# Keys and values of two heads as paired products, with the block sums and the early logits moved

## The chip, the cores and the metric

The kernel runs on one core of one Trainium2 chip. A core has a matrix engine (TensorE, PE in the profile, with its weight loads as PEld), a vector engine (VectorE, DVE), a scalar engine (ScalarE, ACT), GpSimd (POOL) and SyncE (SP), which here only issues transfers. The metric is the device time of one execution in microseconds (us), over three runs of the kernel before: 1576.21, 1579.66 and 1579.71, so the median is 1579.66 us. The profile is of one further execution.

## The reference

One inference step of one decoder layer. A prompt of 512 tokens (16 learned tokens in front, 528 in all) and 8 decoding sequences of 4 tokens each (32) pass through the same weights, so every projection has 560 rows.

```
h = RMSNorm(x)
[q,k,v,ga | cb,cc,ch,gc | ma,mc] = h @ w_in              # 2048 -> 12288
a = StickBreakingAttn(q,k,v) * silu(ga)                  # 8 heads of 128
c = cb * conv3_causal(cc * ch) * silu(gc)
m = sigmoid(ma + b_ga) * (a @ w_pa) + sigmoid(mc + b_gc) * (c @ w_pc)
y = x + RMSNorm(m @ w_out)
A[t,s] = sigmoid(z_ts) * prod_{s<j<t} (1 - sigmoid(z_tj)),  z = q.k / sqrt(128) + b_head
```

The prompt attends to itself. The decoding tokens attend to 512 cached positions each, four pages of 128 positions from a paged cache, and to their own sequence. Keys and values of all rows are outputs too. Everything is float32.

## The kernel before

**Products.** Each float32 operand is split into a high part and a low part: ACT copies the high part (`whi`, L242), DVE subtracts it from the operand (`wlo`, L243), and PE multiplies high by high, high by low and low by high, so every product of 128 rows takes three matmuls. The normed input stands in `h_hi` and `h_lo`, 16 blocks of 128 rows by 560 columns; its columns are cut in two halves of 280. The weights come as tiles of 1024 by 128 over the SP queue into five buffers (`raw`), and the split tiles have three buffers each (`whi`, `wlo`).

**A plain projection** (`proj`, L258) of 128 columns of `w_in` has two weight tiles and 16 x 3 x 2 = 96 matmuls of 280 columns. Queries use 272 columns of each half.

**A pair** (`pair` and `seven`, L983) makes 256 columns of `w_in` as a 2 by 2 block product in seven products instead of eight (Winograd's form). Each product has 8 x 3 = 24 matmuls. It needs sums of weight blocks (four additions on DVE, L1002 to L1020), and sums of the blocks of `h`: three tiles `t_hi`, `t_lo` pairs, and the block (0,1) of `h` itself is replaced by a sum. The four results leave PSUM one after the other.

**Order of stages.** First the norm and the first queries. Then `head_now` for heads 0 to 3: keys, values, the query projection of head h+4, and the attention of head h for the prompt (`attend`: scores L623, softplus on ACT and DVE, suffix sums on PE L705, exponentials L711, values L717). The attention's tiles lie in the pool `now`. Then `head_later` for heads 4 to 7: keys and values are made and stored for later. Then the block sums (L948 to L968, on DVE and ACT), which are in a pool of their own (`tsum`). The six tiles `t_hi`, `t_lo` are taken right after the pool `now` is given back, on the same side of the memory: 52 KB a partition that stand where `now` (51,968 bytes a partition) stood. From there everything that reads `h` is a pair: 4 pairs for `ga`, 16 for the convolution, 16 for the gates `ma` and `mc` (L1127 to L1156). Then attention of heads 4 to 7 beside `c @ w_pc`, then `a @ w_pa`, `w_out` and the final norm.

**Decoding beside this.** `decode_steps` is a generator. Its first part makes the logits of the cached keys on DVE: 16 units, each with four pages, each page with 16 dot products of 128 by 128 (`junk`, L784). So there are 64 of them in a unit and 1024 in all. The first six units (`DEC1`) run beside heads 0 to 3, in a pool that must be closed before the pool `tsum` opens; the other ten run beside `ga`, the convolution and the first gates (`dec_group` after each pair, numbered n = 1 to 36; the first loads are issued after the second `ga` pair). When all logits are there, two steps make their softplus on ACT (L469 to L472) and the suffix sums; the next makes the exponentials, and then come the values.

**What sets the order.** The instructions of each engine are put in an order when the program is built, by a planner that follows the written order where several are ready and lets later work go ahead where nothing earlier is. On the chip each engine then keeps that order. `pin` (also `keep_in_program_order`) holds an instruction behind the one written before it on its engine; `issue_after` holds a group behind a named one. The sigmoids of the gates (L1145) that are written after a softmax step stand behind the last ACT instruction of that step (L1144), and the step stands behind the four sigmoids written before it (`behind_gates`), so that the ACT tables change seldom.

Of the kernel before, what the change touches and what calls it, by code (L numbers as in the profile page):

```python
# [17 lines left out]
P = 128  # L18
# [28 lines left out]
EPS = 1e-6  # L47
DEC1 = 6
SCRATCH = 4096
FIRST = 4  # L50
WARM = 10
NOW = 4
LNEXP = "natural_log_exp_and_others"
SCALE = P ** -0.5
# [6 lines left out]
def hybrid_step_kernel(  # L61
# [176 lines left out]

    def w_split(x):
        hi = whl.tile([P, 8, P], F32R, tag="hi", name="whi")  # L240
        lo = whl.tile([P, 8, P], F32R, tag="lo", name="wlo")
        act.copy(hi, x)  # L242
        low[0] = dve.tensor_sub(lo, x, hi.bitcast(F32))  # L243
        return hi, lo
# [258 lines left out]

    def natural(raw, nat, nat_s):
# [8 lines left out]
        dve.tensor_copy(nat[0:16, 4, :], pt[0:16, 0:P])  # L513
        dve.tensor_copy(nat_s, pt[0:TS, P:2 * P])

# [47 lines left out]

    def k_proj(h):
        o = proj(GATE_K + h * P, ALL)
        kr = hp.tile([P, T], F32, name="raw", bufs=2)
        for ob, s in nparts(o):
            act.copy(kr[:, s], ob)
        kn = hp.tile([P, 5, P], F32, name="nat", bufs=2)
        ks = hp.tile([TS, P], F32, name="ks", bufs=1)  # L570
        natural(kr, kn, ks)
        outputs(k_prompt, k_sample, h, kn, ks, pin if h == 0 else lambda x: x)

        zz = z_ps()[0:TS, 0:TS]
        pe.matmul(zz, lhsT=kr[:, TP:T], rhs=qs_all[:, h, :], start=True, stop=True)
# [4 lines left out]
    def v_proj(h, pl=None):  # L580
        o = proj(GATE_V + h * P, ALL)
        vr = hp.tile([P, T], F32, name="raw", bufs=2)
        for ob, s in nparts(o):
            act.copy(vr[:, s], ob)
        vn = hp.tile([P, 5, P], F32, name="nat", bufs=2)
        vs = hp.tile([TS, P], F32, name="ks", bufs=1)
        natural(vr, vn, vs)
        outputs(v_prompt, v_sample, h, vn, vs)
        pool.dma_start(v_scr[:, h * P:(h + 1) * P], vs)
        if pl is None:  # L590
            pool.dma_start(vn_scr[h][0:512].rearrange("(a p) d -> p a d", p=P), vn[:, 0:4, :])
            pool.dma_start(vn_scr[h][512:TP], vn[0:16, 4, :])
            return None
        return v_split(pl, vn)

# [8 lines left out]
    def attend(pl, h, khi, klo, vhi, vlo, qhi, qlo, pl_a=None, after=None, between=None):  # L604
# [114 lines left out]
        yield ot  # L719

    def head_now(h):

        qr = hp.tile([P, TQ], F32, name="qr", bufs=2)[:, 0:PQ]
        nc.sync.dma_start(qr, qt_scr[h][:, 0:PQ])
        khi, klo = k_split(np_, k_proj(h))
        dec_step(1 if h else 0, "part")
        vhi, vlo = v_proj(h, np_)
        dec_step(1, "part")
        q_proj(NOW + h)
        dec_step(2, "part")  # L730
        ot = next(attend(np_, h, khi, klo, vhi, vlo, *q_split(np_, qr)))
        dec_step(2, "part")
        at = np_.tile([P, PQ], F32, name="at", bufs=1)
        act.copy(at, ot)
        pool.dma_start(a_scr[h], at)

    def head_later(h):
        pool.dma_start(k_scr[h], k_proj(h))
        dec_step(2, "part")
        v_proj(h)  # L740
        dec_step(2, "part")

# [183 lines left out]
    nctx.close()  # L926
    for h in range(NOW, H):
        head_later(h)
    dec_step(64, "part")
# [5 lines left out]
    for i in range(3):  # L935
        ttp = tctx.enter_context(tc.tile_pool(name=f"tt{i}", bufs=1))
        t_hi.append(ttp.tile([P, 8, HU], F32R, name=f"t_hi{i}"))
        t_lo.append(ttp.tile([P, 8, HU], F32R, name=f"t_lo{i}"))
    h_f, l_f = h_hi.bitcast(F32), h_lo.bitcast(F32)

    def blk(x, i, j):
        return x[:, 8 * i:8 * i + 8, (j + 1) * HC - HU:(j + 1) * HC]

    def t_split(hi, lo, x):
        act.copy(hi, x)
        dve.tensor_sub(lo, x, hi.bitcast(F32))

    with tc.tile_pool(name="tsum", bufs=2, side="right") as tsp:  # L948
        r1 = tsp.tile([P, 8, HU], F32, name="r1", bufs=1)
        for c in range(0, 8, 2):  # L950
            def part(x, *ij):
                return (blk(x, *ij) if ij else x)[:, c:c + 2]

            r, x, y = part(r1), *(tsp.tile([P, 2, HU], F32, name=n) for n in "xy")
            dve.tensor_sub(r, part(h_f, 0, 0), part(h_f, 0, 1))
            dve.tensor_add(r, r, part(l_f, 0, 0))
            dve.tensor_sub(r, r, part(l_f, 0, 1))
            dve.tensor_add(x, r, part(h_f, 1, 1))
            dve.tensor_add(x, x, part(l_f, 1, 1))
            t_split(part(t_hi[0]), part(t_lo[0]), x)  # L960
            dve.tensor_sub(y, part(h_f, 0, 0), x)
            dve.tensor_add(y, y, part(l_f, 0, 0))
            t_split(part(t_hi[1]), part(t_lo[1]), y)
            dve.tensor_sub(x, part(h_f, 1, 0), x)
            dve.tensor_add(x, x, part(l_f, 1, 0))
            t_split(part(t_hi[2]), part(t_lo[2]), x)
        for c in range(0, 8, 2):
            t_split(blk(h_hi, 0, 1)[:, c:c + 2], blk(h_lo, 0, 1)[:, c:c + 2], r1[:, c:c + 2])  # L968
    hctx.close()
# [63 lines left out]
    def pair(c, n):  # L1033
# [6 lines left out]
        def rt(i):  # L1040
            return lambda k: (t_hi[i][:, k, HU - n:HU], t_lo[i][:, k, HU - n:HU])

        ws = blocks_of(win, c)
        s = sp2.tile([P, 8, P], F32, name="s")
        yield from seven(ws, n, rb, rt, s, lambda name: sp2.tile([P, HU], F32, name=name)[:, :n])

    gctx, uctx = ExitStack(), ExitStack()
    sp2 = gctx.enter_context(tc.tile_pool(name="sums", bufs=1))
    gp = gctx.enter_context(tc.tile_pool(name="gates", bufs=2))
    up_ = uctx.enter_context(tc.tile_pool(name="convu", bufs=2))  # L1050
# [89 lines left out]
    for j in range(0, KD, 2):  # L1140
        for w, c in ((0, COL_MA), (1, COL_MC)):
# [384 lines left out]
```

## Time and profile before

| what | value |
|---|---|
| median of three runs | 1579.66 us (1576.21 to 1579.71) |
| the profiled execution | 1577.78 us, span 1576.2 us |
| mean granted TensorE clock | 0.993 |
| PE busy | 1560.4 us, 99% of the span |
| PEld busy | 1526.9 us, 97% |
| DVE busy | 1261.6 us, 80% |
| ACT busy | 753.5 us, 48% |
| POOL busy | 236.2 us, 15% |

The span runs from the first to the last instruction; the execution's own time is 1.6 us longer. Times within the profile are counted from the start of the span. Matmuls are pipelined, so the duration of one (289 ns on average for 272 columns) is not what it costs: that is the distance from one start to the next. A wait is charged to the instruction that came last, as far as the profile can tell.

### The profile page before, as it was taken

How to read it: one execution, taken by the hardware profiler on the slowest of the kernel's cores; microseconds unless marked ns; L12 is line 12 of the kernel's file. 1: busy time of each engine (PE TensorE's matmuls, PEld its weight loads, DVE VectorE, ACT ScalarE, POOL GpSimd, SP SyncE). 2: the span in 40 equal slices, each digit the busy share in tenths (PEclk: the TensorE clock that was granted, in tenths of full speed). 3: DMA queues.
4: the chain of work that ended last, by engine and by line, in shares of the span. 5: the costliest groups of instructions: out<-in, count | busy, mean ns of one | idle time of the engine just before them, and what ended most of it. 6: DMA issues, size and time to landing. Idle time of an engine off the chain costs nothing.

```text
span 1576.2 us, 32342 instructions
## 1 busy us (share of the span) xinstructions
PE 1560.4 (99%) x12172; PEld 1526.9 (97%) x12172; DVE 1261.6 (80%) x3574; ACT 753.5 (48%) x1339; POOL 236.2 (15%) x428
## 2 busy tenths in 40 slices
PE   8999999999999999999999999999999999999997
PEld 8999999999999999999999999898899999999997
DVE  7328999965799999999999996655678857877686
ACT  6235555434444444344444465444476733445562
POOL 1133333222111011011011113212100010000000
PEclk8999999999999999999999999999999999999999
DMA  8245556344564445445355547667595465443345
GB/s 256 86 135 179 165 169 184 107 125 141 155 189 128 143 141 156 134 142 168 108 172 174 168 131 239 188 190 229 156 310 181 129 187 170 148 115 88 102 142 186
DMA packets 300674, 252.77 MB, mean 160 GB/s; under 512 B 11521, under 2 KB 268613, under 8 KB 299701
## 3 DMA queue, kind: packets, MB, share of 16 engines
q1 hardware_dynamic: 272021, 160.45, 35.4%
q0 software_dynamic: 28368, 89.98, 17.2%
q8 instruction: 95, 1.56, 0.4%
q14 instruction: 62, 0.51, 0.1%
q10 hardware_dynamic: 128, 0.27, 0.1%
HBM read 217.95 MB, written 32.71 MB: 159 GB/s over the span
## 4 chain that ended last, share of the span: by engine, by line
PE 97%; DVE 2%; ACT 1%; issue 0%; DVEq 0%; ACTq 0%
PE mm L983 33%; PE mm L258 28%; PE o L983 24%; PE mm L323 2%; PE z L705 1%; PE o L717 1%; PE z L323 1%; PE tp L859 1%; PE z L623 1%; PE z L1467 1%; PE tp L508 0%; PE z L1321 0%; DVE wlo L243 0%; PE tp L158 0%; DVE junk L784 0%; PE z L216 0%
## 5 line engine op out<-in xcount | busy, mean ns | idle before, releaser
L242 ACT CAST whi<-raw 128x1024 fp32r<-128x1024 f32 x247 | 259.2, 1050 | 339.6 <-PE mm L983 96.7
L243 DVE TENSOR_TENSOR wlo<-raw,whi 128x1024 fp32r<-128x1024 f32 x247 | 301.9, 1223 | 106.6 <-ACT whi L242 104.3
L983 PE MATMUL mm<-h_hi,whi 128*128 128x272 f32 (+1 forms) x1152 | 333.1, 289 | 0.2 <-ACT whi L242 0.2
L983 PE MATMUL mm<-h_lo,whi 128*128 128x272 f32 (+1 forms) x1152 | 332.7, 289 | 0.0
L983 PE MATMUL mm<-h_hi,wlo 128*128 128x272 f32 (+1 forms) x1152 | 331.7, 290 | 0.1
L983 PE MATMUL o<-t_hi,whi 128*128 128x272 f32 (+1 forms) x864 | 250.2, 290 | 0.0
L983 PE MATMUL o<-t_lo,whi 128*128 128x272 f32 (+1 forms) x864 | 249.9, 289 | 0.0
L983 PE MATMUL o<-t_hi,wlo 128*128 128x272 f32 (+1 forms) x864 | 249.7, 289 | 0.0
L784 DVE CUSTOM_DVE_ANT_0 junk<-kpage,qb 128x128 f32<-128x128 f32 x1024 | 245.6, 287 | 2.9 <-DMA qb<-q_scr 2.4
L983 PEld LDWEIGHTS mm<-h_hi,whi 128*128 128x128 f32 x1152 | 217.4, 189 | 7.2 <-ACT whi L242 3.8
L983 PEld LDWEIGHTS mm<-h_hi,wlo 128*128 128x128 f32 x1152 | 216.6, 189 | 1.3 <-DVE wlo L243 0.8
L983 PEld LDWEIGHTS mm<-h_lo,whi 128*128 128x128 f32 x1152 | 216.8, 188 | 0.1
L242 ACT CAST whi<-s 128x1024 fp32r<-128x1024 f32 x126 | 132.1, 1048 | 150.0 <-PE mm L983 50.4
L243 DVE TENSOR_TENSOR wlo<-s,whi 128x1024 fp32r<-128x1024 f32 x126 | 153.9, 1221 | 61.2 <-ACT whi L242 61.0
L258 PE MATMUL mm<-h_lo,whi 128*128 128x280 f32 (+1 forms) x640 | 187.6, 293 | 0.0
L258 PE MATMUL mm<-h_hi,wlo 128*128 128x280 f32 (+1 forms) x640 | 187.1, 293 | 0.0
L258 PE MATMUL mm<-h_hi,whi 128*128 128x280 f32 (+1 forms) x640 | 186.7, 292 | 0.0
L983 PEld LDWEIGHTS o<-t_hi,wlo 128*128 128x128 f32 x864 | 163.1, 189 | 0.7 <-DVE wlo L243 0.7
L983 PEld LDWEIGHTS o<-t_lo,whi 128*128 128x128 f32 x864 | 163.4, 189 | 0.0
L983 PEld LDWEIGHTS o<-t_hi,whi 128*128 128x128 f32 x864 | 162.9, 189 | 0.1
L258 PEld LDWEIGHTS mm<-h_lo,whi 128*128 128x128 f32 x640 | 120.3, 188 | 0.8
L258 PEld LDWEIGHTS mm<-h_hi,whi 128*128 128x128 f32 x640 | 120.5, 188 | 0.5
(448 smaller groups left out, 3165.9 us busy)
## 6 DMA issues: line engine op xcount, KB each, us to landing
raw<-in_w_in SPq DMA_DIRECT2D x192, 512.0 KB, 4.3
kpage<-in_cache_k POOLq DMA_DIRECT2D x64, 256.0 KB, 3.6
qb<-q_scr POOLq DMA_DIRECT2D x32, 512.0 KB, 5.6
vpage<-in_cache_v POOLq DMA_DIRECT2D x64, 256.0 KB, 6.1
raw<-in_w_out SPq DMA_DIRECT2D x32, 512.0 KB, 4.0
gate_scr<-g POOLq DMA_DIRECT2D x32, 272.0 KB, 3.5
gt<-gate_scr POOLq DMA_DIRECT2D x16, 544.0 KB, 4.0
raw<-in_w_pc SPq DMA_DIRECT2D x16, 512.0 KB, 4.6
```

What stands on the lines that cost most here:

```text
L242: act.copy(hi, x)
L243: low[0] = dve.tensor_sub(lo, x, hi.bitcast(F32))
L258: pe.matmul(o, lhsT=w, rhs=r[:, t0:t1], start=(k == 0 and n == 0), stop=(k == nk - 1 and n == 2))
L323: pin(pe.matmul(o, lhsT=l, rhs=r[:, k, t0:t1], start=(start and m == 0), stop=(stop and m == 2), skip_group_check=True))
L623: pe.matmul(zt[:m, c0:c0 + n], lhsT=l[:, s0:s0 + m], rhs=r[:, ts:ts + n], start=(c0 == 0 and i == 0), stop=(i == 2), skip_group_check=True)
L705: pe.matmul(o, lhsT=l, rhs=x, start=False, stop=(i == len(ops) - 1), skip_group_check=True)
L717: pe.matmul(ot[:, ts - NMETA:ts - NMETA + n], lhsT=l[:m, st, :], rhs=x[:m, c0:c0 + n], start=False, stop=(g == GROUPS[-1] and i == 2), ski ...
L784: dve.tensor_tensor_reduce(out=junk, in0=kt[:, h * P:(h + 1) * P], in1=qt[:, t, h * P:(h + 1) * P], scale=1.0, scalar=0.0, op0=ALU.mult, o ...
L859: pin(pe.matmul(po[32 * j:32 * (j + 1), :], lhsT=lhs, rhs=rhs, start=(pg == 0), stop=last and n >= len(vts) - 4, tile_position=(0, 32 * j) ...
L983: pe.matmul(o, lhsT=l[:, k, :], rhs=r, start=(start and k == 0 and m == 0), stop=(stop and k == 7 and m == 2), skip_group_check=True)
L1467: pin(pe.matmul(o, lhsT=(m1, m2)[h][:, k + 8 * (q == 1), ts], rhs=two[h][q == 2][:, :, k, :], start=(n == 0), stop=(n == 47)))
```

## The change

Heads 4 and 5 keep plain projections. The keys of heads 6 and 7 become one pair, their values another, on all 280 columns of each half (`later_pair`); the `t` tiles therefore grow from 274 to 280 columns. The pairs come after the block sums and before the `ga` pairs.

The block sums are rewritten and put between the four projections of heads 4 and 5, one quarter (`t_sums`) after each: every DVE instruction of them is pinned, and so are the low parts of the weights from the second projection on. Copies to the natural layout that DVE made for heads 4 and 5 go to ACT.

`DEC1` is 5 instead of 6: one unit of logits goes from beside heads 0 to 3 to beside the gates. `PAGES` says how many pages are written after each part of `head_now`. `dec_group` has one more group with four pages (n = 26), and the softmax step comes at n = 27 instead of 26. The mask tile `after` moves to another pool.

```diff
-DEC1 = 6
+DEC1 = 5
+SOLO = 6
...
-    def w_split(x):
+    def w_split(x, pin=lambda ins: ins):
...
-        low[0] = dve.tensor_sub(lo, x, hi.bitcast(F32))
+        low[0] = pin(dve.tensor_sub(lo, x, hi.bitcast(F32)))
...
+    PAGES = ((1, 1, 2, 2), (1, 1, 2, 1), (1, 1, 2, 1), (1, 1, 1, 1))
...
+    def later_pair(c, h, qs=None):
+
+        raws = [hp2.tile([P, T], F32, name="raw", bufs=2) for _ in range(2)]
+        seen = []
+        for m, half, b in pair(c + h * P, HC):
+            act.copy(raws[m][:, NMETA + half * HQ:NMETA + (half + 1) * HQ], b[:, HM:])
+            act.copy(raws[m][:, half * HM:(half + 1) * HM], b[:, :HM])
+            seen.append(m)
+            if seen.count(m) < 2:
+                continue
+            if qs is not None:
+                k_store(h + m, raws[m])
+                k_out(hp2, h + m, raws[m], qs[:, m, :])
+            else:
+                v_store(h + m, v_out(hp2, h + m, raws[m]))
...
-        if n <= 25:
+        if n <= 26:
             dec_step((0, 2, 2, 2)[n - 1] if n <= 4 else 1 if n <= 20 else 4, "logits")
         else:
-            dec_step(2 if n in (26, 28) else 1)
+            dec_step(2 if n in (27, 28, 29) else 1)
...
     nctx.close()
-    for h in range(NOW, H):
-        head_later(h)
     dec_step(64, "part")
...
     def t_split(hi, lo, x):
         act.copy(hi, x)
-        dve.tensor_sub(lo, x, hi.bitcast(F32))
+        pin(dve.tensor_sub(lo, x, hi.bitcast(F32)))
...
+        def t_sums(c):
...
+            def whole(out, *ij):
+                pin(dve.tensor_add(out, part(h_f, *ij), part(l_f, *ij)))
...
+            whole(y, 0, 0)
+            whole(r, 0, 1)
+            pin(dve.tensor_sub(r, y, r))
+            whole(x, 1, 1)
+            pin(dve.tensor_add(x, r, x))
+            pin(dve.tensor_sub(y, y, x))
             t_split(part(t_hi[0]), part(t_lo[0]), x)
+            z = tsp.tile([P, 2, HC], F32, name="z", bufs=1)
+            whole(z, 1, 0)
             t_split(part(t_hi[1]), part(t_lo[1]), y)
+            pin(dve.tensor_sub(z, z, x))
+            t_split(part(t_hi[2]), part(t_lo[2]), z)
+
+        tiles = [c + h * P for h in range(NOW, SOLO) for c in (GATE_K, GATE_V)]
...
+        units = {(0, u): unit(0, u) for u in range(2)}
+        for i, c in enumerate(tiles):
+            h = NOW + i // 2
+            if i:
+                units[i, 1] = unit(i, 1, pin)
+            o = gemm([units[i, u] for u in range(2)], h_rhs, ALL)
+            t_sums(2 * i)
+            if i + 1 < len(tiles):
+                units[i + 1, 0] = unit(i + 1, 0, pin)
+            else:
+                for c in range(0, 8, 2):
+                    t_split(blk(h_hi, 0, 1)[:, c:c + 2], blk(h_lo, 0, 1)[:, c:c + 2], r1[:, c:c + 2])
+            raw = raw_of(o)
...
+        qs = hp2.tile([P, H - SOLO, TS], F32, name="qs")
+        for h in range(SOLO, H):
+            pool.dma_start(qs[:, h - SOLO, :], qt_scr[h][:, PQ:TQ])
+        later_pair(GATE_K, SOLO, qs)
+        later_pair(GATE_V, SOLO)
```

More of the change, by code (lines that the diff above doesn't have):

```diff
@@ L502, in split_evac, with natural @@
                                      op0=ALU.mult, op1=ALU.subtract)
-    def natural(raw, nat, nat_s):
+    def natural(raw, nat, nat_s, copy=dve.tensor_copy):
         pt = t_ps()
@@ L562, in v_split, with raw_of, k_out, k_proj @@
         return vhi, vlo
-    def k_proj(h):
-        o = proj(GATE_K + h * P, ALL)
-        kr = hp.tile([P, T], F32, name="raw", bufs=2)
+    def raw_of(o):
+        raw = hp.tile([P, T], F32, name="raw", bufs=2)
         for ob, s in nparts(o):
-            act.copy(kr[:, s], ob)
+            act.copy(raw[:, s], ob)
+        return raw
+    def k_out(hp, h, kr, qs, copy=dve.tensor_copy):
         kn = hp.tile([P, 5, P], F32, name="nat", bufs=2)
         ks = hp.tile([TS, P], F32, name="ks", bufs=1)
-        natural(kr, kn, ks)
+        natural(kr, kn, ks, copy)
         outputs(k_prompt, k_sample, h, kn, ks, pin if h == 0 else lambda x: x)
         zz = z_ps()[0:TS, 0:TS]
-        pe.matmul(zz, lhsT=kr[:, TP:T], rhs=qs_all[:, h, :], start=True, stop=True)
+        pe.matmul(zz, lhsT=kr[:, TP:T], rhs=qs, start=True, stop=True)
         act.activation(z_new[:, :, h, :], zz.rearrange("p (b t) -> p b t", t=DT), AF.Identity,
                        bias=bsb[0:TS, h:h + 1])
-        return kr
[L580 to L584, printed above, removed]
+    def k_proj(h):
+        kr = raw_of(proj(GATE_K + h * P, ALL))
+        k_out(hp, h, kr, qs_all[:, h, :])
+        return kr
+    def v_out(hp, h, vr, copy=dve.tensor_copy):
         vn = hp.tile([P, 5, P], F32, name="nat", bufs=2)
         vs = hp.tile([TS, P], F32, name="ks", bufs=1)
-        natural(vr, vn, vs)
+        natural(vr, vn, vs, copy)
         outputs(v_prompt, v_sample, h, vn, vs)
         pool.dma_start(v_scr[:, h * P:(h + 1) * P], vs)
[L590 to L594, printed above, removed]
+        return vn
+    def v_proj(h):
+        return v_out(hp, h, raw_of(proj(GATE_V + h * P, ALL)))
+    def k_store(h, kr):
+        pool.dma_start(k_scr[h], kr)
+    def v_store(h, vn):
+        pool.dma_start(vn_scr[h][0:512].rearrange("(a p) d -> p a d", p=P), vn[:, 0:4, :])
+        pool.dma_start(vn_scr[h][512:TP], vn[0:16, 4, :])
     def q_split(pl, qr):
@@ L725, in head_now @@
         khi, klo = k_split(np_, k_proj(h))
-        dec_step(1 if h else 0, "part")
-        vhi, vlo = v_proj(h, np_)
-        dec_step(1, "part")
+        dec_step(PAGES[h][0], "part")
+        vhi, vlo = v_split(np_, v_proj(h))
+        dec_step(PAGES[h][1], "part")
         q_proj(NOW + h)
-        dec_step(2, "part")
+        dec_step(PAGES[h][2], "part")
         ot = next(attend(np_, h, khi, klo, vhi, vlo, *q_split(np_, qr)))
-        dec_step(2, "part")
+        dec_step(PAGES[h][3], "part")
         at = np_.tile([P, PQ], F32, name="at", bufs=1)
@@ new lines, in t_sums, with unit @@
+            t_split(part(t_hi[2]), part(t_lo[2]), z)
+        tiles = [c + h * P for h in range(NOW, SOLO) for c in (GATE_K, GATE_V)]
+        def unit(i, u, pin=lambda ins: ins):
+            return w_split(w_load(win_srcs(tiles[i])[u]), pin)
+        units = {(0, u): unit(0, u) for u in range(2)}
[11 more added lines that the diff above has]
+            raw = raw_of(o)
+            if i % 2 == 0:
+                k_store(h, raw)
+                k_out(hp, h, raw, qs_all[:, h, :], act.copy)
+            else:
+                v_store(h, v_out(hp, h, raw, act.copy))
@@ L1040, in rt @@
         def rt(i):
-            return lambda k: (t_hi[i][:, k, HU - n:HU], t_lo[i][:, k, HU - n:HU])
+            return lambda k: (t_hi[i][:, k, HC - n:], t_lo[i][:, k, HC - n:])
         ws = blocks_of(win, c)
         s = sp2.tile([P, 8, P], F32, name="s")
-        yield from seven(ws, n, rb, rt, s, lambda name: sp2.tile([P, HU], F32, name=name)[:, :n])
+        yield from seven(ws, n, rb, rt, s, lambda name: sp2.tile([P, HC], F32, name=name)[:, :n])
     gctx, uctx = ExitStack(), ExitStack()
     sp2 = gctx.enter_context(tc.tile_pool(name="sums", bufs=1))
+    with tc.tile_pool(name="heads2", bufs=1) as hp2:
+        qs = hp2.tile([P, H - SOLO, TS], F32, name="qs")
[3 more added lines that the diff above has]
+        later_pair(GATE_V, SOLO)
     gp = gctx.enter_context(tc.tile_pool(name="gates", bufs=2))
```

36 lines of the change are left out of this document (9 added, 27 removed).

## The prediction

> **What bounds the kernel now.** I read the page first: the busy times and the chain that ended last.
>
> ```profile
> span 1576.2 us, 32342 instructions
> PE 1560.4 (99%) x12172; PEld 1526.9 (97%) x12172; DVE 1261.6 (80%) x3574; ACT 753.5 (48%) x1339; POOL 236.2 (15%) x428
> ...
> PE 97%; DVE 2%; ACT 1%; issue 0%; DVEq 0%; ACTq 0%
> ```
>
> PE is the bound and almost the only one: 97% of the chain is PE. So an edit helps only as far as PE gets fewer matmuls, and any wait that PE is given is paid in full. Busy time is not cost with pipelined matmuls; the cost of one is read from the chain in order of time, where a run of matmuls without a gap is one piece.
>
> ```profile
> 309.02 9.24 PE mm L258 x72
> ...
> 388.80 6.04 PE mm L983 x48
> ```
>
> The first piece is a plain projection with 280 columns, 9.24 / 72 = 128.3 ns each; the second is a pair with 272, 6.04 / 48 = 125.8 ns.
>
> How near is PE to waiting? For that I took the waits of the weight loads between 366 and 925 us (the pairs), and then the stages by window.
>
> ```profile
> PEld mm L983 <- DVE wlo L243: 0.8, 4, 0.4
> PEld o L983 <- DVE wlo L243: 0.7, 4, 0.2
> PEld mm L983 <- ACT whi L242: 0.4, 1, 0.4
> ```
>
> These three rows are all: 1.9 us in 559. Yet DVE is nearly full there. One `ga` pair without logits and one gate pair with them, all engines (PE, PEld, DVE, ACT, POOL):
>
> ```profile
> 388.64:409.77 21.13, 21.13 (x170) 21.13 (x169) 13.93 (x16) 9.65 (x14) 0.64 (x3) 1.00 0.42 126
> ...
> 900.92:922.07 21.15, 21.15 (x170) 21.15 (x169) 20.13 (x76) 9.92 (x15) 1.09 (x2) 1.00 0.44 127
> ```
>
> DVE needs 13.9 us for a pair, and the dot products fill it to 20.1 of 21.15. PE doesn't wait because the dots are put between the low parts. That decides below.
>
> **The products.** Keys and values of heads 6 and 7 are 4 projections of 96 matmuls, 384; two pairs of seven products are 2 x 7 x 24 = 336. 48 fewer at 128.3 ns: **-6.2 us**. Transposes to the natural layout are as many as before. Weights too: eight tiles of 512 KB on SP. DVE makes 14 low parts and 8 weight sums for the two pairs in place of 8 low parts; a pair's DVE time is the 13.9 us above beside some 21.6 of PE, so that is covered. Results leave PSUM by ACT (9.65 of 21.13 busy): covered too.
>
> **The block sums beside heads 4 and 5.** They are 48 DVE instructions now, 52 before, of some 0.72 us, and 11 of them follow each projection:
>
> ```profile
> L946 DVE TENSOR_TENSOR t_lo<-y,t_hi 128x548 fp32r<-128x548 f32 x4 | 2.9, 713 | 0.0
> ...
> L945 ACT CAST t_hi<-y 128x548 fp32r<-128x548 f32 x4 | 2.6, 651 | 0.2 <-DVE y L962 0.2
> ...
> L243 DVE TENSOR_TENSOR wlo<-raw,whi 128x1024 fp32r<-128x1024 f32 x247 | 301.9, 1223 | 106.6 <-ACT whi L242 104.3
> ```
>
> 11 x 0.72 and two low parts of 1.22 are 10.4 us of DVE against 96 x 0.128 = 12.3 of PE, so from the second projection on they keep up. If each of a quarter's three splits waited 0.65 for ACT, it would be 12.3, just even. I count 0 (bounds 0 and 3 us). What isn't covered is the first quarter. The low part of the first weights of V4 (the values of head 4) is pinned behind `t_sums(0)`, which writes `t_lo0` and others. These stand where `now` stood: by the shapes, `t_lo0` lies on `vhi` and `vlo` of head 3's attention, `t_lo2` on its result `at`. So DVE waits there until the values' matmuls of head 3 have ended, and until `at` is stored; behind it on DVE are the rest of the quarter and V4's low part, and PE waits for that.
>
> In the kernel before, nothing like it was in the way. Here are the ends of projections on ACT (K4 at 270.1, V4 at 286.2, the first half of K5 at 294.6) and the first scores and last values of head 3 on PE:
>
> ```profile
> 270.13 0.44 ACT L568 COPY raw<-mm 128x272 f32<-128x272 f32 x2
> ...
> 286.21 0.40 ACT L584 COPY raw<-mm 128x272 f32<-128x272 f32 x1
> ...
> 293.17 0.59 ACT L734 COPY at<-o 128x512 f32<-128x512 f32 x1 [1.29 <-PE o L717]
> 294.58 0.46 ACT L568 COPY raw<-mm 128x272 f32<-128x272 f32 x2 [0.82 <-PE mm L258]
> ```
>
> ```profile
> 254.31 0.34 PE L623 MATMUL z<-qhi,khi 128*128 128x400 f32 x1
> ...
> 292.73 0.40 PE L717 MATMUL o<-hiA,vlo 128*128 128x512 f32 x1
> ```
>
> PE was full through the 38.8 us of that attention because K4, V4 and 36 matmuls of K5 filled it. Now only K4 can. Without V4 (96), those 36 and V4's transposes (0.4), PE's own work up to the end of the attention is done at 293.1 - 132 x 0.1283 - 0.4 = 275.8.
>
> When does that attention end? DVE has fewer dots beside it: the dots alone, in the windows of heads 0 and 3, are
>
> ```profile
> 117.10:154.40 37.30, 16.62 (x69) 1.00 0.58 178
> ...
> 254.30:293.10 38.80, 20.76 (x89) 1.00 0.46 139
> ```
>
> 295 of the 384 (six units of 64) were done by 254.3; at that pace 25 of 320 are left for head 3, 64 fewer, 64 x 20.76 / 89 = 14.9 us. If all of it came off the attention, it would end at 278.2; if nothing did, at 293.1. The rows above say little did: 20 dots fewer in head 0 made 1.5 us, which for 64 is 4.8, an end at 288.3. But three low parts (V4's, K5's first) are away too. I take the middle of 278 and 288, **283**.
>
> After that end, `at` takes 0.6, its store is issued 0.3 later and lands in
>
> ```profile
> a_scr<-at POOLq DMA_DIRECT2D x4, 256.0 KB, 3.0
> ```
>
> with 0.56 for the issue: 4.5 us, then `t_lo2` 0.7 and V4's low part 1.2. V4 starts 6.4 us after the attention, at 289.4, instead of 275.8: **+13.6 us** (bounds 8.8 with 278.2, 23.7 with 293.1). A gain is excluded, since PE has no idle time to lose here.
>
> **After a standstill** PE's clock is lower. In the only late stretch in which PE stands, it is the column behind POOL's:
>
> ```profile
> 1560.00:1576.20 16.20, 5.43 (x46) 5.23 (x44) 10.45 (x23) 1.47 (x6) 2.10 (x4) 0.77 0.76 274
> ```
>
> 0.23 of 5.43 us: **+1.2 us** for a standstill (bounds 0 and, from the start of the run at 0.72 over 16.55 busy, 4.6).
>
> ```profile
> 0.00:20.00 20.00, 16.55 (x76) 13.96 (x77) 12.98 (x31) 13.00 (x21) 0.99 (x7) 0.72 0.91 260
> ```
>
> [...]
>
> **The early logits.** A unit is 64 dots; 704 instead of 640 now lie beside the pairs, from the same place on (the first loads are pinned behind the second `ga` pair). The dots alone in the last three windows of pairs before the softmax:
>
> ```profile
> 879.78:900.92 21.14, 7.27 (x31) 1.00 0.50 151
> 900.92:922.07 21.15, 7.25 (x31) 1.00 0.44 127
> 922.07:945.28 23.21, 0.78 (x3) 1.00 0.51 151
> ```
>
> 31 a pair, and the last three dots fall into the very pair before whose first sigmoid the softmax must be done. 64 more are 2.06 pairs, but the softmax is written only one pair later, so it comes 1.06 pairs, 22.4 us, later against the sigmoids that are held behind it. How much of that is free? On ACT, before:
>
> ```profile
> 924.32 1.05 ACT L242 CAST whi<-s 128x1024 fp32r<-128x1024 f32 x1 [0.26 <-DVE s L1005]
> ...
> 936.80 0.71 ACT L472 ACTIVATE dr<-z_all,zero_c 128x512 f32<-128x512 f32 x1
> 937.52 1.28 ACT L1145 ACT_TABLE_LOAD   x1
> 938.82 0.49 ACT L1145 ACTIVATE g<-mm,bg 128x272 f32<-128x272 f32 x1
> ```
>
> That sigmoid frees one of three PSUM buffers at 939.3. PE needs it for the second product of the next pair, 945.3 + 24 x 0.126 = 948.3: 9.0 us free, so 13.4 remain. While PE stands, the softmax goes faster: five copies of weights (1.05 each) that lay between its instructions are not there, and the last dots don't share DVE. I take off 7.4 and leave **+6.0 us** (bounds 13.4, and 0 if dots fill the 1 us a pair that DVE is idle). The lower clock follows: **+1.2**. Beside heads 0 to 3 the 64 dots that go bring nothing themselves, as PE was full there. POOL has two small loads more (`qs`), and the unit's six loads move with it; it is 15% busy.
>
> **Sum**: -6.2 + 13.6 + 1.2 + 6.0 + 1.2 = +15.8, so 1577.8 + 15.8 = **1594** us. The base is the profiled execution, 1577.78; it is 1.9 below the median of the three runs and within them.
>
> **Rivals.**
> - *Only the first wait.* The dots find room: DVE's idle 1 us a pair takes 4 to 5 more, and two gate pairs more would do. Against: the count stays at 31 although 1 us is free. -6.2 + 13.6 + 1.2: 1586.
> - *Only the second.* The tiles `t` are not held by the attention, since head 3 ends before K4 does. It would have to end by 269, 9 us below my bound, or be begun before Q7, the last query projection. -6.2 + 7.2: 1579, no change.
> - *PE stays fed (the other side).* The order is made anew with 15 us less on DVE ahead of head 3. If its scores come before Q7 (96 x 0.126 = 12.1 us) and not behind it, Q7 fills PE beside that attention, the wait of 13.6 shrinks to about 1.5, and the dots go into DVE's idle time. For: PE waited 1.9 us in 559 though DVE was 95% busy, so this planner keeps PE fed. Against: Q7 is written first, and was first before. It decides from 7.4 us of fill on, where the first wait and its clock are worth no more than the products. With all of it hidden: 1577.8 - 6.2 = 1572.
> - *DVE bound through the pinned quarters*, so that the stage doesn't give what it says: up to 3 us more, inside the range.
>
> **Chances.** Both waits 0.42; only the first 0.24; only the second 0.13; PE fed 0.21. A measurement of this kernel can tell 0.3%, 4.7 us, from no change. Faster by more is PE fed but for a rest of it with small waits: 0.18. Within it lie that rest and the case of only the second wait: 0.15. Slower: 0.67. The upper bounds together give -6.2 + 23.7 + 13.4 + 2.4 = +33, 1611, but the two seldom come together; I stop at 1603. Below, the range must hold the case without waits, 1572, with a little under it: 1570. The forecast's own range is 1586 to 1603.
>
> **What would show it.** The products: 384 fewer and 336 more matmuls, 128 ns apart. The first wait: a gap on PE of some 9 to 24 us between K4 and V4, ended by `wlo`, behind a DVE wait at a `t_lo`. The second: PE standing in the second product some 28 pairs after the first `ga` pair, ended by a sigmoid, and fewer than 33 dots a pair. The clock column below 1.00 behind either. I am wrong if PE has no gap over 2 us between 270 and 300, or if the dots end within the pair after n = 26.

## The result and the profile after

The changed kernel takes 1599.62 us (median of four runs, 1599.15 to 1603.64); the kernel before, on the same chip, 1579.68. The ratio is 1.0145 with a 95% interval of 1.0133 to 1.0157: **slower by 1.45%**, some 21 us. The forecast was 1594 with a range of 1570 to 1603. The profiled execution took 1599.15 us, 21.4 more than that of the kernel before.

The page's head, its chain, and of its strips those of PE and of PE's clock, all of the changed kernel:

```profile
span 1597.5 us, 32289 instructions
...
PE 1560.2 (98%) x12124; PEld 1524.5 (95%) x12124; DVE 1276.6 (80%) x3580; ACT 763.5 (48%) x1359; POOL 238.6 (15%) x430
...
PE   8999999799999999999999997999999999999997
...
PEclk8999999899999999999999998999999999999998
...
PE 91%; DVE 3%; issue 2%; DMA 1%; ACT 1%; POOLq 1%; POOL 1%; DVEq 0%; ACTq 0%
```

PE has 12124 instructions instead of 12172: the 48 fewer are there. PE's busy time, 1560.2 us, hardly moved, and its share of the chain fell from 97 to 91%. The strips have two dents that the kernel before doesn't have, in the eighth slice of 40 us and in the 25th, and the clock has them too. PE's waits, the two longest of the kernel (in total, times, longest):

```profile
PE mm L259 <- DVE wlo L244: 9.5, 1, 9.5
PE z L851 <- POOL dS L826: 8.8, 1, 8.8
```

**The first standstill.** Last values matmul of head 3 on PE, and the first matmul of V4 that needs a low part (its first two, with the high part alone, ran before); then ACT, POOL and DVE between them (start, duration, in brackets the idle time before and what ended it):

```profile
281.46 0.63 PE L726 MATMUL o<-hiA,vlo 128*128 128x512 f32 x1
291.55 0.60 PE L259 MATMUL mm<-h_hi,wlo 128*128 128x280 f32 x1 [9.46 <-DVE wlo L244]
```

```profile
282.12 0.59 ACT L745 COPY at<-o 128x512 f32<-128x512 f32 x1 [3.94 <-PE o L726]
285.50 0.66 ACT L964 CAST t_hi<-x 128x560 fp32r<-128x560 f32 x1 [2.79 <-DMA a_scr<-at]
```

```profile
283.01 0.57 POOL L746 DMA_DIRECT2D a_scr<-at  x1 [5.69 <-ACT at L745]
```

```profile
286.19 0.74 DVE L965 TENSOR_TENSOR t_lo<-x,t_hi 128x560 fp32r<-128x560 f32 x1 [7.28 <-ACT t_hi L964]
...
289.62 0.74 DVE L965 TENSOR_TENSOR t_lo<-z,t_hi 128x560 fp32r<-128x560 f32 x1 [0.72 <-ACT t_hi L964]
290.27 2.35 DVE L244 TENSOR_TENSOR wlo<-raw,whi 128x1024 fp32r<-128x1024 f32 x2
```

The attention ends at 282.1, its result `at` is copied and stored, and only when that store has landed does ACT write the first `t_hi`. Five DVE instructions of the quarter and V4's low part follow; V4 goes on at 291.55.

**The second standstill.** The stretch with the last dots (DVE busy and count on `junk` alone), then PE, POOL and ACT around it:

```profile
953.15:974.27 21.12, 7.52 (x32) 1.00 0.43 126
974.27:977.45 3.18, 1.00 (x4) 1.00 0.01 2
```

```profile
977.16 0.29 PE L1029 MATMUL mm<-h_hi,wlo 128*128 128x272 f32 x1
986.28 1.06 PE L851 MATMUL z<-dS,neg_u 32*32 32x256 f32 x2 [8.83 <-POOL dS L826]
```

```profile
985.13 1.10 POOL L826 TENSOR_SCALAR_AFFINE_SELECT dS<-dS 32x256 f32<-32x256 f32 x1
```

```profile
978.36 0.50 ACT L470 ACTIVATE de<-z_new,zero_c 32x256 f32<-32x256 f32 x1
...
986.17 0.71 ACT L473 ACTIVATE dr<-z_all,zero_c 128x512 f32<-128x512 f32 x1
986.90 1.28 ACT L1197 ACT_TABLE_LOAD   x1
988.19 0.49 ACT L1197 ACTIVATE g<-mm,bg 128x272 f32<-128x272 f32 x1
```

The last dots fall into the pair in which the softmax must be done; the softmax takes ACT, DVE and POOL from 977 to 986. The instruction that PE has next in its order is not a product but the decode's suffix sum (L851), which needs POOL's mask; the products behind it wait too.

Where the 21.4 us lie, by the start of K3 (the keys of head 3), of the first `ga` pair, and of the 26th and 36th pair from there on:

| stretch | before | after | difference |
|---|---|---|---|
| up to K3 | 210.3 | 211.2 | +1.0 |
| K3 to the first `ga` pair | 156.5 | 166.1 | +9.6 |
| 25 pairs | 534.1 | 533.6 | -0.6 |
| 10 pairs around the softmax | 237.0 | 248.4 | +11.3 |
| from there to the end | 438.2 | 438.3 | +0.0 |

The differences are taken before rounding. Up to K3 the two kernels do not have the same code: 194 dots stand ahead of K3 before, 217 after.

### The profile page after: what moved, and what is told of

It reads as the page before. It is cut to its first block, busy times and chain, and to the rows that moved or that the text cites. A ratio compares the mean times of both kernels' runs of the same rounds, so it can differ in the third digit from the quotient of the medians.

```text
span 1597.5 us, 32289 instructions
## 1 busy us (share of the span) xinstructions
PE 1560.2 (98%) x12124; PEld 1524.5 (95%) x12124; DVE 1276.6 (80%) x3580; ACT 763.5 (48%) x1359; POOL 238.6 (15%) x430
## 4 chain that ended last, share of the span: by engine, by line
PE 91%; DVE 3%; issue 2%; DMA 1%; ACT 1%; POOLq 1%; POOL 1%; DVEq 0%; ACTq 0%
PE mm L1029 35%; PE o L1029 25%; PE mm L259 21%; PE mm L324 1%; PE z L324 1%; PE tp L880 1%; PE z L714 1%; PE o L726 1%; POOLq L780 1%; PE z L632 1%; PE z L1519 1%; DVE wlo L244 0%; PE tp L509 0%; PE z L1373 0%; DVE junk L805 0%
## 5 line engine op out<-in xcount | busy, mean ns | idle before, releaser
L1029 PE MATMUL mm<-h_hi,whi 128*128 128x272 f32 (+2 forms) x1216 | 352.6, 290 | 0.0
L1029 PE MATMUL mm<-h_lo,whi 128*128 128x272 f32 (+2 forms) x1216 | 351.3, 289 | 0.0
L1029 PE MATMUL mm<-h_hi,wlo 128*128 128x272 f32 (+2 forms) x1216 | 351.2, 290 | 0.1
L1029 PE MATMUL o<-t_hi,wlo 128*128 128x272 f32 (+2 forms) x912 | 264.2, 290 | 0.0
L1029 PE MATMUL o<-t_hi,whi 128*128 128x272 f32 (+2 forms) x912 | 264.0, 289 | 0.0
L1029 PE MATMUL o<-t_lo,whi 128*128 128x272 f32 (+2 forms) x912 | 263.1, 288 | 0.0
L1029 PEld LDWEIGHTS mm<-h_hi,whi 128*128 128x128 f32 x1216 | 230.0, 189 | 4.3 <-ACT whi L243 2.5
L1029 PEld LDWEIGHTS mm<-h_lo,whi 128*128 128x128 f32 x1216 | 229.3, 189 | 1.8 <-issue 1.7
L1029 PEld LDWEIGHTS mm<-h_hi,wlo 128*128 128x128 f32 x1216 | 229.0, 189 | 1.8 <-DVE wlo L244 0.8
L259 PEld LDWEIGHTS mm<-h_hi,wlo 128*128 128x128 f32 x512 | 97.0, 190 | 10.8 <-DVE wlo L244 10.2
L259 PE MATMUL mm<-c_hl,whi 128*128 128x272 f32 x512 | 100.3, 288 | 0.0
```

The source lines that it names most:

```text
L259: pe.matmul(o, lhsT=w, rhs=r[:, t0:t1], start=(k == 0 and n == 0), stop=(k == nk - 1 and n == 2))
L1029: pe.matmul(o, lhsT=l[:, k, :], rhs=r, start=(start and k == 0 and m == 0), stop=(stop and k == 7 and m == 2), skip_group_check=True)
```

## The experiments

In all of them positions are counted from the start of K3 on PE, since the profiled executions reach K3 at times from 210.3 to 214.7 us. But for the kernel before and e8, PE, DVE and ACT have the same instructions in the same order up to there. The table is read from the timelines: "values" is the end of head 3's values, "first t" the start of the first `t_lo`, "last h" the end of the last `h_lo` of the block sums, "pair" the second product of the first pair (with a dash where the pair's products stand in another order), "ga" the start of the first `ga` pair, "softmax" the ten pairs of the table above.

| kernel | ratio to before (95%) | values | first t | last h | pair | ga | softmax |
|---|---|---|---|---|---|---|---|
| before | 1 | 82.9 | | | | 156.5 | 237.0 |
| after | 1.0145 (1.0133 to 1.0157) | 70.8 | 75.0 | 121.5 | 123.6 | 166.1 | 248.4 |
| e1 softmax later | 1.0084 (1.0068 to 1.0101) | 71.2 | 75.3 | 122.3 | 124.5 | 166.9 | 238.4 |
| e2 `at` apart | 1.0139 (1.0122 to 1.0156) | 71.2 | 72.5 | 117.2 | 121.4 | 163.9 | 248.6 |
| e3 Q7 behind | 1.0144 (1.0127 to 1.0161) | 69.9 | 74.0 | 121.0 | 123.1 | 165.6 | 248.7 |
| e4 logits alone | 1.0088 (1.0071 to 1.0105) | 89.3 | | | | 156.6 | 249.1 |
| e5 V4 first | 1.0137 (1.0120 to 1.0153) | 78.2 | 82.3 | 133.0 | - | 165.7 | 247.8 |
| e6 both waits | 1.0083 (1.0059 to 1.0108) | 78.2 | 79.4 | 120.0 | 122.5 | 167.1 | 238.2 |
| e7 dots early | 1.0072 (1.0055 to 1.0089) | 71.2 | 75.3 | 122.5 | 124.6 | 167.1 | 236.8 |
| e8 six units | 1.0086 (1.0069 to 1.0102) | 76.1 | 80.3 | 127.0 | 129.1 | 171.6 | 236.8 |
| e9 attention sooner | 1.0029 (1.0018 to 1.0039) | 67.1 | 68.3 | 112.1 | 116.3 | 158.8 | 238.1 |
| e10 sooner, V4 first | 1.0027 (1.0016 to 1.0039) | 68.7 | 70.0 | 112.1 | 114.5 | 160.2 | 237.8 |
| e11 light sums | 1.0034 (1.0022 to 1.0046) | 76.5 | 77.7 | 112.4 | 115.2 | 160.0 | 238.5 |
| e12 sums ahead | 1.0005 (0.9995 to 1.0015) | 68.7 | 70.7 | 106.9 | 110.1 | 154.9 | 237.0 |

### The second standstill: e1, e4, e7, e8

e1 writes the softmax one group later:

```diff
-        if n <= 26:
+        if n <= 27:
...
-            dec_step(2 if n in (27, 28, 29) else 1)
+            dec_step(2 if n in (28, 29, 30, 31) else 1)
```

> The changed kernel with the softmax steps one group later (first at n = 28 instead of 27), nothing else. Two-waits theory: the standstill of 9.1 us at 977 and the slow matmuls behind it go, since 31 more dots have room before the softmax; 1599.6 - 11 = 1588 to 1589 us, no gap of PE over 2 us between 960 and 1020. Rival: the standstill belongs to the order (the decode's suffix matmul stands ahead of products on PE, wherever the softmax is written); then it moves one pair later and the time stays at 1597 to 1600.

The ratio falls from 1.0145 to 1.0084. The ten pairs take 238.4 us, 10.0 less, and PE doesn't stop there: 15.00 us busy of 15.00 at the place where it stood.

```profile
975.00:990.00 15.00, 15.00 (x121) 15.00 (x121) 14.72 (x32) 11.47 (x19) 1.08 (x2) 1.00 0.55 166
```

So the order on PE is not enough to make a standstill: with dots that end a pair ahead of the softmax, the suffix sum finds its input in time. The 1.3 us that stay against the kernel before are about the size of a new wait of 1.5 us in these pairs, for pages of values, which are loaded later now.

```profile
PE tp L880 <- DMA vpage<-in_cache_v: 1.5, 1, 1.5
```

e4 puts the logits part of the change alone into the kernel before (`DEC1` = 5, `PAGES`, one more group, softmax at n = 27).

> The kernel before with the logits part of the change alone (DEC1 = 5, PAGES, one more group, softmax at n = 27); no pairs for heads 6 and 7, block sums as before. Two-waits theory: the second standstill alone, 1579.7 + 11 = 1591 us, and no gain from the 64 dots that left heads 0 to 3, since PE was full there. Rival: the second standstill needs the pairs of heads 6 and 7 ahead of it; then 1579 to 1581.

Ratio 1.0088, and the ten pairs take 249.1 us, 12.0 more than before, behind the same wait, with no pair of heads 6 and 7 in the kernel:

```profile
PE z L832 <- POOL dS L807: 8.8, 1, 8.8
```

The first `ga` pair starts where it did before (156.6 against 156.5): the 64 dots that left heads 0 to 3 brought nothing there. Head 3's values even end 6.4 us later than before.

e7 leaves the softmax where the change put it and begins the dots sooner, beside the pairs of heads 6 and 7:

```diff
             if seen.count(m) < 2:
                 continue
+            if m:
+                dec_step(2, "logits")
```

> The changed kernel with four pages of logits written beside the two pairs of heads 6 and 7 (two pages behind each), softmax at n = 27 as in the changed kernel; nothing else. If the second standstill comes from 64 dots that had no room before the softmax: dots begin about two pairs earlier, 62 of them there, and the standstill at 977 goes: 10 to 11 us less than the changed kernel, ratio 1.008. Rival: the place of the softmax in the written order decides, not the dots' end: ratio 1.0145.

Ratio 1.0072; the ten pairs take 236.8 us, and nothing is left of the second standstill. e1 moves the softmax and e7 the dots, and both take it away: it is the distance between the two that decides, one pair too short.

e8 undoes the move of the logits alone (`DEC1` = 6, the pages, groups and softmax of the kernel before).

> The changed kernel with DEC1 = 6 and the pages, groups and softmax (n = 26) of the kernel before, so without the move of the logits. Two-waits theory: the second standstill is gone (11 us less), but 64 more dots delay the end of head 3's attention by 12 to 15 us, and the gap ahead of V4 grows from 10 to 22 to 25: ratio 1.014 to 1.018, as the changed kernel or slower. Rival: head 3's attention isn't held by dots: its end stays at 282, only the second standstill goes: ratio 1.008.

Ratio 1.0086, between the two theories. The second standstill is gone (236.8). The attention of head 3 ends 5.3 us later than in the changed kernel (76.1 against 70.8), not 12 to 15, and the `ga` pairs start 5.5 later. So moving the unit gained 5.5 us at the block sums and cost 11.6 at the softmax.

### The first standstill: e2, e3, e5, e6

e2 puts the tile `at` into another pool than the one that the `t` tiles follow:

```diff
-        at = np_.tile([P, PQ], F32, name="at", bufs=1)
+        at = hp.tile([P, PQ], F32, name="at", bufs=1)
```

> The changed kernel with the tile `at` of heads 0 to 3 in the pool `heads` instead of `now`, nothing else. If the first t write waits because the pool `now` is given back as a whole, and its last user is the store of `at`: the first t_hi starts 0.5 us behind the end of head 3's values (at 282.6 instead of 285.5), V4 2.9 us earlier, 1596.7 us. Rival: each t tile waits only for what lay in its place, as the prediction had it: only t_lo2 lay on `at`, and another instruction of the attention holds the first write; 0 to 1 us of gain, 1599.

```profile
284.10 0.59 ACT L745 COPY at<-o 128x512 f32<-128x512 f32 x1 [4.34 <-PE o L726]
284.58 0.66 ACT L964 CAST t_hi<-x 128x560 fp32r<-128x560 f32 x1
```

The first `t_hi` now follows the copy at once, and the wait of V4 is 6.6 us instead of 9.5. By the shapes `t_hi0` didn't lie on `at`, yet it waited for its store: it seems that in the changed kernel the pool `now` comes free as a whole. No run moved another tile to test that. The `ga` pairs start 2.3 us sooner; against a ratio with an interval of 0.17% on either side, 1.0139 can't be told from 1.0145.

e3 writes the last query projection behind head 3's attention:

```diff
-        q_proj(NOW + h)
+        if h < 3:
+            q_proj(NOW + h)
...
         pool.dma_start(a_scr[h], at)
+        if h == 3:
+            q_proj(NOW + h)
```

> The changed kernel with the last query projection (Q7) written behind head 3's attention instead of ahead of it, nothing else. Two-waits theory: the scores come about 12 us earlier, the attention ends near 271 to 274 with Q7 beside it, and the gap of 10.1 us ahead of V4 falls to 0 to 3; the slow matmuls behind it go too: 1587 to 1591 us. Rival: DVE is bound by the quarters themselves and not by the attention's end, so that V4 starts no earlier than before against K4: 1597 to 1600.

A miss. The scores of head 3 start 13.7 us sooner (first row changed kernel, second row e3), but the values end less than 1 us sooner, and V4 waits 9.5 us as before.

```profile
255.30 0.34 PE L632 MATMUL z<-qhi,khi 128*128 128x400 f32 x1
```

```profile
241.61 0.35 PE L632 MATMUL z<-qhi,khi 128*128 128x400 f32 x1
...
280.40 0.63 PE L726 MATMUL o<-hiA,vlo 128*128 128x512 f32 x1
```

One reason is DVE, in the window between the two starts (columns PE, PEld, DVE, ACT, POOL; first row changed kernel, second row e3):

```profile
241.60:255.30 13.70, 13.70 (x107) 13.24 (x106) 13.06 (x85) 4.47 (x9) 2.86 (x5) 1.00 0.27 84
```

```profile
241.60:255.30 13.70, 13.70 (x105) 13.03 (x104) 13.17 (x82) 10.20 (x21) 2.87 (x5) 1.00 0.26 82
```

DVE was full there with the dots, and it stays full: an attention that may start sooner gets little of DVE. It is not the only reason, as e9 will show. This also corrects a step of mine. I had 25 dots left beside head 3; in the changed kernel there is none, the last dot starts at 44.0, where the scores start (44.1). The dots took DVE's free time in the heads before.

e5 splits both weight tiles of the next projection ahead of the quarter, so that V4 doesn't stand behind it:

```diff
-            if i:
-                units[i, 1] = unit(i, 1, pin)
             o = gemm([units[i, u] for u in range(2)], h_rhs, ALL)
+            for u in range(2 if i + 1 < len(tiles) else 0):
+                units[i + 1, u] = unit(i + 1, u, pin)
             t_sums(2 * i)
-            if i + 1 < len(tiles):
-                units[i + 1, 0] = unit(i + 1, 0, pin)
```

> The changed kernel with both weight tiles of the next projection split ahead of each quarter of the block sums instead of one ahead and one behind it; nothing else. Two-waits theory: V4's low parts no longer stand behind the quarter, so V4 (96 x 0.128 = 12.3 us) runs in the gap; K5 waits 3 us for the first quarter instead: about 10 to 12 us less than the changed kernel, a ratio to before of 1.007 to 1.008. Rival: DVE is bound behind the gap (45 of 58 us busy up to the first pair), so that the gap comes back ahead of the first pairs: less than 4 us, ratio 1.012 or more.

A miss again, for the rival: ratio 1.0137. V4 does run in the gap, but now its matmuls stand between head 3's on PE, and the first sums, which DVE did at the start of head 3's attention, stand in the middle of it; the values end 7.4 us later (78.2). K5 waits 7.9 us where V4 waited 9.5, and three waits in the first pairs are new:

```profile
PE mm L259 <- DVE wlo L244: 7.9, 1, 7.9
...
PE o L1027 <- ACT s L1056: 1.7, 1, 1.7
PE mm L1027 <- ACT whi L243: 1.6, 2, 1.0
```

e6 puts e1, e2 and e5 together.

> The same as e5, with `at` in the pool `heads` and the softmax one group later (e1, e2 and e5 together). If the two standstills are all that the change costs, only the 48 matmuls fewer are left: 6 us below before, ratio 0.996, no gap of PE over 2.5 us between 270 and 1020. Rival: further waits, or slower pairs of heads 6 and 7 (their pieces take 22.3 and 23.7 us), eat the gain: ratio 1.000 or above.

Ratio 1.0083: only the gain of e1. The first pair starts 8.4 us sooner than in the changed kernel and then stands:

```profile
PE mm L1027 <- ACT whi L243: 6.5, 2, 5.9
PE mm L259 <- DVE wlo L244: 3.9, 1, 3.9
```

DVE at that place:

```profile
331.37 0.74 DVE L965 TENSOR_TENSOR t_lo<-z,t_hi 128x560 fp32r<-128x560 f32 x1 [0.93 <-ACT t_hi L964]
332.03 2.69 DVE L965 TENSOR_TENSOR h_lo<-r,h_hi 128x560 fp32r<-128x560 f32 x4
334.75 1.23 DVE L1046 TENSOR_TENSOR s<-raw 128x1024 f32<-128x1024 f32 x1
```

The second product needs the replaced block of `h` and a weight sum, and DVE has them last. This gave a new theory: what binds is not V4 but the way from the end of head 3's attention over the release of `now` to the last `h_lo`, 40 to 47 us of DVE's work and waits (50.7 in e5; in the changed kernel DVE is busy 40.0 of the 46.7 us from the first `t_lo` on). In the changed kernel PE, with V4 late, comes to the second product at the same time, 2.1 us behind the last `h_lo`, so that taking one limit away only shows the other.

### The chain of the block sums: e9 to e12

e11 tests it directly. It is e6 with the block sums made from the high parts alone; the low parts of `h` are left out of them, and so are four DVE instructions of each quarter, 16 x 0.72 = 11.5 us:

```diff
-            whole(y, 0, 0)
-            whole(r, 0, 1)
-            pin(dve.tensor_sub(r, y, r))
-            whole(x, 1, 1)
-            pin(dve.tensor_add(x, r, x))
-            pin(dve.tensor_sub(y, y, x))
+            pin(dve.tensor_sub(r, part(h_f, 0, 0), part(h_f, 0, 1)))
+            pin(dve.tensor_add(x, r, part(h_f, 1, 1)))
+            pin(dve.tensor_sub(y, part(h_f, 0, 0), x))
...
-            whole(z, 1, 0)
-            pin(dve.tensor_sub(z, z, x))
+            pin(dve.tensor_sub(z, part(h_f, 1, 0), x))
```

> As e6, but the block sums are made from the high parts alone, so four DVE instructions fewer in each quarter (16 in all, 16 x 0.72 = 11.5 us of DVE). The low parts are left out of these sums. If DVE's sums bind behind the release, the gap of 6.2 us inside the first pair goes and ga begins 6 to 9 us sooner against e6: ratio 1.003 to 1.004. Rival: what ate e6's gain is something else in the pairs of heads 6 and 7 (transposes, copies, weights): ratio 1.008 as e6.

Ratio 1.0034, as the theory said; `ga` starts 7.1 us sooner than in e6 (160.0 against 167.1), and the wait in the first pair is 2.0 us instead of 6.5:

```profile
PE mm L1023 <- ACT whi L243: 2.0, 2, 1.4
```

The chain from the first `t_lo` to the last `h_lo` takes 34.7 us instead of 40.6: DVE has 11.5 us less to do there and at its start, but waits longer. The pairs of heads 6 and 7 themselves are not what ate e6's gain.

e9 lets the chain begin sooner: Q7 behind the attention as in e3, and this time 64 dots fewer beside heads 0 to 3 (`DEC1` = 4, one page after each part), which are made up for by e7's early dots and e1's later softmax; `at` as in e2.

> The changed kernel with a sooner end of head 3's attention and the second standstill undone: Q7 written behind that attention (as e3), one unit of logits fewer beside heads 0 to 3 (DEC1 = 4, one page after each part), four pages beside the pairs of heads 6 and 7 (as e7), softmax at n = 28 (as e1), `at` in the pool `heads` (as e2). Theory now: ga begins when DVE has done the block sums, 40 to 47 us behind the release of `now`, and the release is the end of that attention; e3 brought nothing because 64 dots took DVE in its place. So the attention ends near 270, 12 us sooner, and the gap ahead of V4 is 5 to 7 us or less: ratio 0.996 to 1.000, 24 us less than the changed kernel. Rival: DVE or the planner stretches the attention to the end of K4 again and something else binds: ratio 1.004 to 1.008, only the second standstill gone.

Ratio 1.0029, just above the range. The values end at 67.1, 3.8 us sooner than in the changed kernel and not 12: on PE they stand behind K4's last matmuls again, so the rival was right in part. DVE has room now, while PE is full:

```profile
241.00:250.00 9.00, 9.00 (x68) 8.35 (x67) 2.83 (x6) 5.23 (x13) 1.34 (x2) 1.00 0.38 117
```

So what holds the attention's end here is PE's own work and order, and more of DVE alone could not have made e3's end much sooner either (67.1 against 69.9). Even so the `t` writes start 6.7 us sooner, the last `h_lo` ends 9.4 sooner, and `ga` starts 7.3 sooner. V4 still waits:

```profile
PE mm L259 <- DVE wlo L244: 6.6, 1, 6.6
```

e10 adds e5's order to e9.

> As e9, with both weight tiles of the next projection split ahead of each quarter (as e5). If the release and DVE's 40 us behind it bind, this changes nothing in the end (the gap ahead of V4 goes, one ahead of the second product of the first pair comes): within 2 us of e9. If PE's own work binds in e9: 5 us less than e9.

Ratio 1.0027, no difference to e9. The wait of V4 is gone altogether, and 6.5 us in the first pair have taken its place:

```profile
PE mm L1032 <- ACT whi L243: 6.5, 2, 5.9
```

Both kernels end their last `h_lo` at 112.1, though the first `t_lo` starts 1.7 us later in e10. That is the theory's clearest row: V4's wait of 6.6 us can be there or not, the chain of the sums ends at the same time.

e12 shortens this chain without leaving anything out. In each quarter all additions come ahead of the three splits, and the first three additions of the next quarter between them, so that DVE doesn't wait for ACT; y gets a tile of full size:

```diff
+            if c == 0:
+                t_begin(c)
+            whole(part, x, 1, 1)
+            pin(dve.tensor_add(x, r, x))
+            pin(dve.tensor_sub(y, y, x))
+            z = tsp.tile([P, 2, HC], F32, name="z", bufs=1)
+            whole(part, z, 1, 0)
+            pin(dve.tensor_sub(z, z, x))
+            if c < 6:
+                t_begin(c + 2)
+            for i, s in enumerate((x, y, z)):
+                t_split(part(t_hi[i]), part(t_lo[i]), s)
```

> As e10, with each quarter's additions written ahead of its three splits and the first three additions of the next quarter between them, so that DVE doesn't wait for ACT inside a quarter and eleven additions more stand ahead of the release or in those waits; the arithmetic is the same, a full-size tile holds y. Theory: in e10 DVE takes 41.6 us from the first t_lo to the last h_lo, 7 of it waits and 3.6 movable; without them the gap of 6.2 us in the first pair goes and ga begins 7 to 9 us sooner than in e10, 152 us behind the start of the last K's products instead of 160: ratio 0.997 to 0.999, faster than the kernel before by 2 to 5 us. Rival: the release moves later by as much (as in e5), so that the ratio stays at 1.002 to 1.003.

Ratio 1.0005 with an interval of 0.9995 to 1.0015: the loss is undone, but nothing is gained that can be measured. Against e10, DVE's way from the first `t_lo` to the last `h_lo` fell from 42.1 to 36.2 us, and `ga` starts 5.3 us sooner, at 154.9, not at 152. What is left of the wait lies behind the sums, in the first pair's own weight sum:

```profile
317.20 1.38 DVE L970 TENSOR_TENSOR h_lo<-r,h_hi 128x560 fp32r<-128x560 f32 x2
318.62 1.23 DVE L1058 TENSOR_TENSOR s<-raw 128x1024 f32<-128x1024 f32 x1
...
321.71 1.23 DVE L244 TENSOR_TENSOR wlo<-s,whi 128x1024 fp32r<-128x1024 f32 x1 [0.60 <-ACT whi L243]
```

`s` stands behind the last `h_lo` on DVE, then come ACT's high part and PE, at 321.73, 1.45 us late. From K3 to the first pair PE has no wait left in e10 and e12 (103.9 us), and in the changed kernel the two pairs take 45.9 with nothing holding them. Together that would be 149.8, 6.7 under the kernel before, which agrees with the 6.2 of the products; no kernel here had both. The 5.1 us that e12 takes more are three waits of PE in the first pair (0.7, 1.4 and 0.7 us) and, for the most part, a clock of 0.50 from 323.5 to 326.9. By its stages e12's profile is 2.5 us faster than that of before behind K3, but the medians of the runs show no gain.

## Why the prediction was right, and where it wasn't

**The sign and the size** came out: the forecast was that both waits arise, 1594, and both did, at 1599.6. By the table of stages the terms measure -6.2 + 15.8 (9.6 and the 6.2 that PE saved) + 11.3, against -6.2 + 14.8 + 7.2 (each wait with its slower clock) in the sum. Both waits came, and both were larger.

**The products**, -6.2: 48 matmuls fewer, as counted. Beside the arithmetic, the stages of e12 and of the changed kernel agree with it (6.7); no run shows it alone.

**The end of head 3's attention**, 283: it was 282.1, but that was luck, since the road was wrong. I expected 25 dots to be left beside head 3, and none was (e3's section). The 4.8 us that I had from head 0's row agrees with e8, where 64 dots move this end by 5.3; in e4, where V4 and K5 still run beside it, the same 64 dots fewer brought an end 6.4 us later. Counted from K3 the attention ended 12.0 us sooner than before. That the rest of them lies with the low parts and projections that no longer stand in it, which I had only named, is likely but not shown.

**From its end to V4**, 6.4 us: it was 9.5 (282.1 to 291.55). I let only `t_lo2` wait for the store of `at`, since only it lies there; the whole pool did, and so the quarter's remaining splits and additions, 4.8 us from the first `t_hi` to V4's low part, came behind the store and not beside it. e2 shows the 2.9 us.

**"I count 0" for the other quarters** is the step whose reasoning failed, though the sum hid it: in the changed kernel PE has no wait between V4 and the first `ga` pair, so the 0 itself holds there. I weighed each quarter's 10.4 us of DVE against a projection's 12.3 of PE, and that holds while PE is late. It says nothing of what happens when PE isn't: then the quarters, the low parts between them and the last splits, 40 to 47 us from the release, are longer than the 37 us of V4, K5 and V5 (3 x 96 x 0.128). So behind V4's wait there was a second limit of nearly the same size, the longer chain, and V4 was only the first that waited for it. e5, e6 and e10 took V4's wait away and the time came back a few steps later; in e5 and e6 the chain itself also began 7 us later, so that e9 beside e10 is the cleaner pair. e11 and e12 shortened the chain and kept what they gained. In the list of rivals "DVE bound through the pinned quarters" was there, with up to 3 us; once V4's wait is gone it is worth nearly all of that wait.

**The clock behind a standstill**, 1.2 us each from POOL's tail of the run: the rows inside the kernel, behind the first and the second standstill, are

```profile
291.50:295.50 4.00, 3.95 (x17) 3.96 (x18) 3.93 (x6) 0.00 (x0) 0.00 (x0) 0.51 0.63 181
295.50:300.00 4.50, 4.50 (x37) 4.50 (x37) 4.03 (x6) 1.73 (x3) 0.00 (x0) 1.00 0.27 72
...
986.30:990.30 4.00, 4.00 (x10) 2.65 (x11) 3.44 (x8) 3.94 (x7) 0.53 (x1) 0.50 0.00 0
```

17 matmuls in 4.0 us are 0.235 each, against 0.128: 17 x 0.107 = 1.8 us for the first, at a clock of 0.51. The term of 1.2, from a stretch at 0.77, was too small. And the clock was 0.50 already in the last values of head 3, ahead of the standstill, and PE's longest wait in that attention up to there had been 1.8 us (changed kernel; the wait, then the window):

```profile
277.09 0.44 PE L726 MATMUL o<-hi,vhi 128*128 128x400 f32 x1 [1.81 <-ACT hi L498]
```

```profile
278.35:282.10 3.75, 3.74 (x13) 2.86 (x12) 0.56 (x1) 0.00 (x0) 0.00 (x0) 0.50 0.00 0
```

Half of these 3.75 us, an estimated 1.9, and 2.7 us of short waits of PE in that attention were in no term of their own. With V4's wait of 9.5 and the 1.8 behind it they make up the 15.8 to within 0.1.

**The second wait**, 6.0: it was 11.3 with the clock, so an estimated 9.5 without it (PE's own wait was 8.8). The count of 31 dots a pair held (31 and 32). The softmax began 41.3 us later behind the first `ga` pair, 20.1 beyond the one pair that it was moved, against 22.4 in the sum. What failed is the 7.4 that I took off because the softmax would go faster while PE stands: from its first to its last ACT instruction it took 8.5 us, against 11.0 before, so only 2.5 came off. It is a chain through ACT, DVE and POOL, and two low parts and a weight sum of the products still lay on DVE in it. And not a sigmoid ended it, as I wrote, but the decode's own suffix sum ahead of the products on PE. The wait lies between the middle and the upper bound of 13.4.

**Rivals.** That only one wait comes is out. "PE stays fed" had the planner put Q7 beside the attention; e3 made that order by hand, and the attention ended 1 us sooner and the time was the same, so this rival would not have come true by that way. The prediction's signs to look for (a gap of 9 to 24 us between K4 and V4 ended by `wlo`, a stop of PE some 28 pairs behind the first `ga` pair, under 33 dots a pair, the clock) came, but for the sigmoid.

## What to carry to other kernels

A wait in the profile names who came last, not how long the way is: before you price or remove one, follow the engine that ends it on to the next point where the bound engine needs it, and compare both ways from their common start. Here two ways ended within some 2 us of each other, and taking away the visible wait three times gave nothing, while taking 11.5 us of work out of the unseen chain gave 7. When work is moved to a later stage, count how far its last piece moves against the first reader that can't move: 64 dots at 31 a pair are two pairs, and the reader was moved by one.

A pool that is given back and taken again can be a dependency on its last reader, a store included, as e2 shows (without it V4's wait was 6.6 us instead of 9.5); a tile that is stored at the end of a stage is better kept in another pool.

## What the runs showed of the hardware

The standstill of PE of 9.5 us cost 1.8 us more behind it, at a granted clock of 0.51 for 4.0 us. The clock had fallen to 0.50 at 278.35, ahead of it, in a stretch with no wait of PE over 1.8 us. Executions in which PE, DVE and ACT have the same instructions up to K3 reached it at 210.49 us (e5) and 214.69 us (e6):

```profile
210.49 0.29 PE L259 MATMUL mm<-h_hi,whi 128*128 128x280 f32 x1
```

```profile
214.69 0.29 PE L259 MATMUL mm<-h_hi,whi 128*128 128x280 f32 x1
```

Of the 4.2 us, 3.5 have arisen in the first 34: the 161st matmul starts at 29.8 in e5 and at 33.4 in e6. Their cause stays open. They are more than the difference between several of these kernels, so a single profile's total can't rank them, and stages counted from a common instruction can.
